# The second product of each attention block on the full array, with k's low part padded by zeros

## The chip, the core and the metric

The kernel runs on one core of a Trainium2 chip. The metric is the device time of one execution in microseconds; the runs shown are whole executions on the chip. The core has five engines that work beside each other, each through its own queue in a fixed order: TensorE (matmuls, and as a second queue the loads of their weights), VectorE, ScalarE, GpSimd and SyncE, which issues the transfers.

## The reference

The reference is an encoder of two layers on 512 tokens with 1024 features, in float32. Each layer has three branches that read the same normed stream: a neighbourhood attention on a 64 wide grid (4 heads), a sliding-window attention (8 query heads on 2 key heads, 128 queries per block), and a gated delta net run in both directions. The branches are projected, gated, added and projected again, and a feed-forward part follows. The change touches the logits of both attentions:

```python
s = jnp.einsum('brqhd,brjkhd->brhqjk', qg, kg).astype(jnp.float32) * (HEAD_DIM ** -0.5)     # neighbourhood
s = jnp.einsum('bnqhgd,bnkhd->bnhgqk', qb, kb).astype(jnp.float32) * (HEAD_DIM ** -0.5)     # sliding window
```

Both contract over the 64 features of a head.

## The kernel before, in words

Tokens lie along the columns and features on the 128 partitions. Every product of float32 values is made in three: a value is split into a rounded high part and a low part that holds the rest, and high x high, high x low and low x high are added in PSUM. For the weights `load_w` does this (lines 133 to 146): a transfer brings a chunk, ScalarE rounds it (line 142), GpSimd subtracts (line 144). `mm3` (lines 148 to 152) issues the three matmuls of 512 columns each; these are the bulk of the kernel's work (lines 150, 151, 152).

For the attentions a head has 64 features, so two heads share the partitions. For each of the two heads, e, `na_project` builds the stationary operand `qp[e]` with the head's q rounded on its own 64 partitions and q's low part on the other 64 (lines 376 and 377), and the moving operand `kh[e]` with k's rounded part on both halves. One product on the full array then gives q high x k high + q low x k high. The third term, q high x k low, is a second matmul into the same PSUM bank. It uses the 64 partitions of that head alone, with `kl`, one tile for both heads (line 380):

```python
T.matmul(sc[:, 0:256], lhsT=q_, rhs=kh[e][:, k1:k1 + 256], start=True, stop=False)
T.matmul(sc[:, 0:256], lhsT=q_[r], rhs=kl[r, k1:k1 + 256], start=False, stop=True)
```

These are lines 418 and 419 in `na_attend`, which runs over 2 pairs of heads, 4 blocks of 128 queries and the 2 heads of a pair: 16 times a layer, always 256 columns. In `swa_attend` lines 508 and 509 do the same for the sliding window, with `qs`, `kdh` and `kdl` from `swa_project`, over 4 query heads of a group, 4 blocks and 2 groups: 32 times a layer, with 256 columns at the ends and 384 between. VectorE then scales, masks and reduces the logits (lines 421 and 512), ScalarE takes the exponentials, TensorE transposes them (lines 430, 431, 530) and multiplies by v on half of the array's columns (lines 437, 534).

The delta net runs beside this. `gdn_cross` doubles k into tiles of the ring `dup` (`doubled`, by ScalarE at line 80), `gdn_solve` inverts the blocks by 31 steps of substitution on VectorE (lines 712 and 714) and transposes them (lines 721 to 727), and hands them to many small matmuls on parts of the array (line 748 on). `gdn_mid` transposes the doubled k (line 782) and the doubled v, which takes tiles of the same ring (lines 799 and 802). `gdn_scan` then goes through 8 steps in which TensorE and VectorE take turns (lines 831, 834, 842, 847). The merge (`merge`) issues the gates' and branches' dense products.

The order in which each engine meets its instructions is not that of the source. The program is traced in the order of the list `ORDER`, and a planner with its own estimates of durations then places instructions on the queues, so that the branches and the merge are mixed. Tiles of one name form a ring with as many buffers as `CAPS` gives; a new tile waits until the last reader of the buffer's old one is done.

Of the kernel before, what the change touches and what calls it, by code (L numbers as in the profile page):

```python
# [7 lines left out]
F32 = mybir.dt.float32  # L8
F32R = mybir.dt.float32r
# [12 lines left out]
# columns of the constant block  # L22
# [3 lines left out]
# columns of the parameter block  # L26
# [3 lines left out]
# chunks of the weight stream  # L30
# [19 lines left out]
CAPS |= {"ysh": 2, "ysl": 2, "kE": 4, "kT": 4, "Q": 4, "VN": 4, "SA": 4, "kq": 4, "dup": 6, "spr": 4, "xo": 4, "qs0": 4, "qs1": 4, "kdh0": 1, "kdh1": 1, "kdl": 1, "nkl": 2, "sv": 1, "hf": 8}  # L50
# [11 lines left out]
def encoder_kernel(ctx, tc, xT, wall, par, cst, nab, out, depth=2, dbg=None):  # L62
# [26 lines left out]
    # rings of 4 KB and 2 KB buffers, one of each for every line of work that runs beside the others  # L89
# [17 lines left out]
    # ---- constants, parameters and small values: one place for each name, or one of a ring  # L107
# [14 lines left out]
    # parameters of a layer  # L122
# [42 lines left out]
    # 1 / sqrt(a) up to the factor RSQ: the halved and inverted exponent as the start, three Newton steps  # L165
# [9 lines left out]
    # sums over the features (their halves), by token: [128, 4, 2]  # L175
# [10 lines left out]
    # values by token, [128, 4, n], brought back over the features  # L186
# [9 lines left out]
    # The residual stream arrives tile by tile: gained and split for the next products, its  # L196
    # squares summed; 1/rms is applied where the products leave PSUM.
# [77 lines left out]
    for l in range(depth):  # L275
# [9 lines left out]
        # raw projections normed over their heads  # L285
# [18 lines left out]
        def perm(a):   # token order (r c) seen as (c r)  # L304
            return a.rearrange("p (r c) -> p c r", r=8)
# [17 lines left out]
        def doubled(src):      # [128, 4, 64] -> the same twice, side by side  # L323
            t = tmp(shape=(128, 4, 2, 64), name="dup")
            (G.tensor_copy(t, src.unsqueeze(2).to_broadcast([128, 4, 2, 64])) if ENG.get("dup") == "G" else copy("dup", t, src.unsqueeze(2).to_broadcast([128, 4, 2, 64])))
            return t
# [11 lines left out]
        def by4(name):      # by chunk and head  # L338
            us = [tmp(shape=(128, 2, 4, 64), name=name) for _ in range(4)]
            return lambda n: us[n // 2][:, n % 2], us  # L340

        def by2(name):      # the same in four parts
            us = [tmp(shape=(128, 4, 2, 64), name=name) for _ in range(4)]
            return lambda n, h: us[n // 4 * 2 + h // 2][:, n % 4, h % 2], us

        def na_project():
            line[0] = "n"
            nonlocal naqk, vt, vt4, rns, irn
            # sums of squares of the stream, permuted
# [10 lines left out]
            for j in range(2):  # L360
                qn, kn = tmp(name="qn"), tmp(name="kn")
                vn = tmp(name="nav")
                acc = dense(l, CH_NA + 3 * j, h)
                S.activation(out=cr(qn), in_=perm(acc), func=AF.Copy, scale=P[:, P_QK:P_QK + 1])
                sq = tmp(name="sq")
                S.activation(out=cr(sq), in_=perm(acc), func=AF.Square)
                pb = sums(sq, halves, "at")
                V.tensor_tensor(anv[:, :, 2 * j:2 * j + 2], mp.unsqueeze(2).to_broadcast([128, 4, 2]),
                                pb, op=ALU.add)
                knorm(permuted(dense(l, CH_NA + 3 * j + 1, h), tmp(name="raw")), P[:, P_QK + 1:P_QK + 2], kn)  # L370
                qp, kh, kl = pair(F32R, name="nqs"), pair(F32R, name="nkh"), tmp(F32R, name="nkl")
                naqk.append((qp, kh, kl))
                for e in range(2):
                    r = slice(64 * e, 64 * e + 64)
                    o = slice(64 - 64 * e, 128 - 64 * e)
                    S.activation(out=qp[e][r], in_=qn[r], func=AF.Copy)
                    on("nql", "G").tensor_tensor(qp[e][o], qn[r], qp[e].bitcast(F32)[r], op=ALU.subtract)
                    copy("nkh", kh[e][r], kn[r], "V")
                    S.activation(out=kh[e][o], in_=kn[r], func=AF.Copy)
                    on("nkl", "V").tensor_tensor(kl[r], kn[r], kh[e].bitcast(F32)[r], op=ALU.subtract)  # L380
                permuted(dense(l, CH_NA + 3 * j + 2, h), vn)
                pt = bank("at")
                for b in range(4):
                    k0, kn0 = (0, 64) if b == 0 else (128 * b - 64, 128)
                    T.transpose(pt[0:kn0, 128 * b:128 * b + 128], vn[:, k0:k0 + kn0], ident)
                S.activation(out=vt[j][0:64, 0], in_=pt[0:64, 0:128], func=AF.Copy)
                S.activation(out=vt[j][:, 1:4], in_=pt[:, 128:512].rearrange("p (b m) -> p b m", b=3), func=AF.Copy)
                pt = bank("at")
                T.transpose(pt[0:64, 0:128], vn[:, 448:512], ident)
                S.activation(out=vt4[0:64, j], in_=pt[0:64, 0:128], func=AF.Copy)  # L390
# [6 lines left out]
        def na_attend():  # L397
            line[0] = "n"
            # ================= neighbourhood attention =================
            for j in range(2):  # L400
                qp, kh, kl = naqk[j]
                py = bank("at")
                for b in range(4):
# [5 lines left out]
                    # the scaled and biased logits negated, and the least of them  # L409
# [4 lines left out]
                    for e in range(2):  # L414
                        r = slice(64 * e, 64 * e + 64)
                        sc = bank("at")
                        q_, k1 = qp[e][:, 128 * b:128 * b + 128], min(k0, 256)
                        T.matmul(sc[:, 0:256], lhsT=q_, rhs=kh[e][:, k1:k1 + 256], start=True, stop=False)
                        T.matmul(sc[:, 0:256], lhsT=q_[r], rhs=kl[r, k1:k1 + 256], start=False, stop=True)
                        c0 = 4 * b + 2 * j + e  # L420
                        V.tensor_tensor_reduce(out=lg[:, e, 0:w], in0=sc[:, k0 - k1:k0 - k1 + w], in1=bias[:, e, 0:w], scale=rns[:, c0:c0 + 1],
                                               scalar=-NEG, op0=ALU.add, op1=ALU.min, accum_out=mx[:, e:e + 1])
# [21 lines left out]
        def swa_project():  # L444
# [5 lines left out]
            kdh, kdl = pair(F32R, name="kdh"), tmp(F32R, name="kdl")  # L450
            for gq in range(2):
# [4 lines left out]
                V.tensor_tensor(kdl[r], kr[r], kdh[gq].bitcast(F32)[r], op=ALU.subtract)  # L456
# [6 lines left out]
            # q stays as projected, times its gain; 1/rms goes into the exponentials  # L463
            qs = []
            aq = kept("aq")      # (b, head of the group, group)
# [23 lines left out]
        def swa_attend():  # L489
            line[0] = "a"  # L490
            # ================= sliding window attention =================
            y["s"] = [None] * 4
            for ep in range(2):
# [3 lines left out]
                for b in range(4):  # L497
# [3 lines left out]
                    for e in range(2):  # L501
                        c0 = 8 * b + 4 * ep + 2 * e
                        mx, sk = small(2, "s", 8), slice(4 * ep + 2 * e, 4 * ep + 2 * e + 2)
                        for gq in range(2):
                            sc = bank("at")
                            q_, kc = qs[2 * ep + e][gq][:, 128 * b:128 * b + 128], slice(128 * kb0, 128 * kb1)
                            r = slice(64 * gq, 64 * gq + 64)
                            T.matmul(sc[:, 0:w], lhsT=q_, rhs=kdh[gq][:, kc], start=True, stop=False)  # L508
                            T.matmul(sc[:, 0:w], lhsT=q_[r], rhs=kdl[r, kc], start=False, stop=True)  # L509
                            # the scaled and masked logits negated, and the least of them and of the sink  # L510
# [30 lines left out]
        def gdn_gates():  # L541
            line[0] = "g"
            nonlocal dec, egn, tlb, gh, gl, beta
            # ================= gated delta net =================
# [3 lines left out]
            # 16 columns beside 512: four parts of the contraction in four column groups, added on the way to the tokens  # L548
# [21 lines left out]
            # beta = 1 / (1 + exp(-b))  # L570
# [4 lines left out]
            # g = -exp(a_log) * (max(a, 0) + log1p(exp(-|a|)))  # L575
# [13 lines left out]
            # cumulative decays  # L589
# [8 lines left out]
            # g split for the decay matrices  # L598
# [5 lines left out]
        def gdn_project():  # L604
            line[0] = "g"
            nonlocal bk, ik, kq, vs, kss, qss
            # k, q, v, twice what the short convolution and silu give. The norms of k and q are applied
            # later: 1/|k| squared in beta, |k| in v, and |q| beside the eps of the output norm.
# [14 lines left out]
            for c in range(2):  # L623
# [9 lines left out]
                if c == 0:  # L633
                    # by token of a chunk, for both directions
# [14 lines left out]
        def gdn_cross():  # L649
            line[0] = "g"  # L650
            nonlocal Q, Qu, Xo, Xg, Lt, Rt, kds, qdec
            # X = beta_j (k_j . k_i) decay, Q = beta_j (q_i . k_j) decay, rows j, columns i
# [4 lines left out]
            for hh in range(4):  # L657
# [24 lines left out]
                # the blocks on the diagonal, column by column, and those beside it  # L682
# [11 lines left out]
        def gdn_solve():  # L694
            line[0] = "g"
            nonlocal W
            # W = (I + X)^-1: the 32-blocks of the diagonal by substitution, one block per lane
# [17 lines left out]
            # back: W[j, i] (forward: R[i, j], backward: R[j, i])  # L715
# [22 lines left out]
            # off-diagonal: W12 = -W11 X12 W22 (forward), W21 = -W22 X21 W11 (backward)  # L738
# [32 lines left out]
        def gdn_mid():  # L771
            line[0] = "g"
            nonlocal kE, kT, wn, VN
            # k and v by token, in both halves of the partitions
# [11 lines left out]
            # wn = -(W' kE)^T rows dk, u = W' v rows i  # L786
# [29 lines left out]
        def gdn_scan():  # L816
            line[0] = "g"
            nonlocal SA
            # scan; VN holds u and then the new values
# [31 lines left out]
        def gdn_z():  # L851
            line[0] = "g"
            nonlocal zs
            # z, twice its silu
# [7 lines left out]
        def gdn_out():  # L862
            line[0] = "g"
            # ---- delta net: outputs, gated RMS norm
# [23 lines left out]
        def merge(i, bn):  # L888
            line[0] = "m"
            # ================= merge =================  # L890
# [49 lines left out]
        # ================= feed forward =================  # L940
# [39 lines left out]
def _w_chunks(w_in, w_bn, w_bs, w_bg, w_out, w_up, w_down):  # L980
# [6 lines left out]
    def put(c, w):      # w: [d, K, 128]  # L987
# [143 lines left out]
```

## Time and profile before

| | |
|---|---|
| median of 3 runs | 1728.22 us (1725.38 to 1728.62) |
| profiled execution: first to last instruction | 1725.9 us |
| TensorE busy | 1685.1 us, 98% |
| weight loads busy | 1329.0 us, 77% |
| VectorE busy | 1009.2 us, 58% |
| GpSimd busy | 832.5 us, 48% |
| ScalarE busy | 743.6 us, 43% |
| mean granted TensorE clock | 0.985 |

The profile comes from one execution. For it the page gives the span from the first to the last instruction and no time around it; the lowest of the runs lies 0.5 us below this span and the median 2.3 us above. A matmul's end in the profile is modelled, so a busy TensorE isn't one at its peak; the distance from one start to the next tells more. In a row, "L509" is line 509 of the kernel, "PE" TensorE, "PEld" its weight loads, "DVE" VectorE, "ACT" ScalarE, "POOL" GpSimd; "64*128 64x256" is a stationary operand of 64 rows and 128 columns and a moving one of 64 rows and 256 columns.

### The profile page before, as it was taken

How to read it: one execution, taken by the hardware profiler on the slowest of the kernel's cores; microseconds unless marked ns; L12 is line 12 of the kernel's file. 1: busy time of each engine (PE TensorE's matmuls, PEld its weight loads, DVE VectorE, ACT ScalarE, POOL GpSimd, SP SyncE). 2: the span in 40 equal slices, each digit the busy share in tenths (PEclk: the TensorE clock that was granted, in tenths of full speed). 3: DMA queues.
4: the chain of work that ended last, by engine and by line, in shares of the span. 5: the costliest groups of instructions: out<-in, count | busy, mean ns of one | idle time of the engine just before them, and what ended most of it. 6: DMA issues, size and time to landing. Idle time of an engine off the chain costs nothing.

```text
span 1725.9 us, 25175 instructions
## 1 busy us (share of the span) xinstructions
PE 1685.1 (98%) x9196; PEld 1329.0 (77%) x9196; DVE 1009.2 (58%) x1809; ACT 743.6 (43%) x1436; POOL 832.5 (48%) x740
## 2 busy tenths in 40 slices
PE   7989999999999999999999999999999999999999
PEld 5766767677888888878886776677778888888887
DVE  5599895434547777741126898855355477777300
ACT  5545544423445444443335564544234354444321
POOL 4664441264544555554448553412644545555543
PEclk9999999999999999999999999999999999999999
DMA  6222221122452332334333221110224623333332
GB/s 209 80 60 75 67 64 36 37 69 70 133 188 87 97 98 98 98 114 132 119 98 95 70 65 49 56 41 29 76 84 143 193 75 96 98 98 98 127 123 74
DMA packets 91500, 160.46 MB, mean 93 GB/s; under 512 B 10352, under 2 KB 17136, under 8 KB 91376
## 3 DMA queue, kind: packets, MB, share of 16 engines
q1 hardware_dynamic: 91376, 158.85, 29.0%
q8 instruction: 72, 1.18, 0.3%
q14 instruction: 52, 0.43, 0.1%
HBM read 147.80 MB, written 8.39 MB: 90 GB/s over the span
## 4 chain that ended last, share of the span: by engine, by line
PE 85%; DVE 9%; issue 2%; ACT 2%; POOL 1%; DMA 1%; SPq 0%; DVEq 0%; POOLq 0%; ACTq 0%
PE mm L152 25%; PE mm L150 24%; PE mm L151 24%; PE at L534 1%; PE at L530 1%; PE at L509 1%; PE at L508 1%; DVE qd L666 1%; PE gd L842 1%; DVE fix L172 1%; DVE fix L170 1%; PE gd L831 1%; PE gd L811 1%; POOL wl L144 1%; DVE lg L427 1%
## 5 line engine op out<-in xcount | busy, mean ns | idle before, releaser
L144 POOL TENSOR_TENSOR wl<-wr,wh 128x512 fp32r<-128x512 f32 (+1 forms) x512 | 686.8, 1349 | 806.8 <-ACT wh L142 754.1
L150 PE MATMUL mm<-hh,wh 128*128 128x512 f32 x1408 | 560.6, 398 | 13.3 <-ACT wh L142 11.7
L152 PE MATMUL mm<-hh,wl 128*128 128x512 f32 x1408 | 561.2, 400 | 1.9 <-POOL wl L144 1.7
L151 PE MATMUL mm<-hl,wh 128*128 128x512 f32 x1408 | 557.2, 396 | 0.0
L142 ACT ACTIVATE wh<-wr 128x512 fp32r<-128x512 f32 (+1 forms) x512 | 314.0, 618 | 402.9 <-PE mm L151 256.1
L150 PEld LDWEIGHTS mm<-hh,wh 128*128 128x128 f32 x1408 | 268.4, 191 | 72.0 <-ACT wh L142 14.3
L152 PEld LDWEIGHTS mm<-hh,wl 128*128 128x128 f32 x1408 | 268.1, 190 | 65.8 <-POOL wl L144 5.7
L151 PEld LDWEIGHTS mm<-hl,wh 128*128 128x128 f32 x1408 | 267.8, 190 | 58.4 <-issue 2.4
L234 DVE SCALAR_TENSOR_TENSOR cv<-up,fix,cv 128x511 f32<-128x511 f32 x88 | 142.0, 1613 | 2.8
L152 PE MATMUL mm<-act,wl 128*128 128x512 f32 x352 | 137.3, 390 | 0.6 <-POOL wl L144 0.6
L150 PE MATMUL mm<-act,wh 128*128 128x512 f32 x352 | 137.2, 390 | 0.3 <-ACT wh L142 0.3
L233 DVE SCALAR_TENSOR_TENSOR cv<-up,fix,cv 128x511 f32<-128x511 f32 x88 | 85.8, 974 | 88.1 <-ACT cv L232 88.1
L151 PE MATMUL mm<-act,wh 128*128 128x512 f32 x352 | 137.1, 389 | 0.0
L970 DVE TENSOR_TENSOR xo<-xo,mm 128x512 f32<-128x512 f32 x16 | 11.0, 687 | 192.1 <-PE mm L152 192.1
L232 ACT ACTIVATE cv<-up,fix 128x512 f32<-128x512 f32 x88 | 70.8, 809 | 34.7 <-DVE up L280 34.7
L162 ACT ACTIVATE act<-cv 128x512 fp32r<-128x512 f32 x44 | 27.8, 632 | 125.8 <-DVE cv L953 125.8
L152 PEld LDWEIGHTS mm<-act,wl 128*128 128x128 f32 x352 | 66.1, 188 | 15.1 <-POOL wl L144 1.5
L150 PEld LDWEIGHTS mm<-act,wh 128*128 128x128 f32 x352 | 66.1, 188 | 14.2 <-ACT wh L142 0.7
L151 PEld LDWEIGHTS mm<-act,wh 128*128 128x128 f32 x352 | 66.1, 188 | 13.8
L952 ACT ACTIVATE cv<-cv 128x512 f32<-128x512 f32 x44 | 27.8, 633 | 85.9 <-DVE cv L234 85.9
L280 DVE TENSOR_TENSOR up<-mm,rstd 128x512 f32<-128x512 f32 x88 | 59.5, 680 | 8.2 <-ACT rstd L228 8.2
L512 DVE CUSTOM_DVE_ANT_0 spr<-at,fix 128x256 f32<-128x256 f32 (+1 forms) x64 | 38.4, 607 | 34.1 <-PE at L509 33.4
(283 smaller groups left out, 2231.7 us busy)
## 6 DMA issues: line engine op xcount, KB each, us to landing
wr<-in_wall_dram SPq DMA_DIRECT2D x496, 256.0 KB, 2.7
xs<-xo SPq DMA_DIRECT2D x24, 256.0 KB, 2.8
xo<-xs SPq DMA_DIRECT2D x24, 256.0 KB, 3.6
xo<-in_xT_dram SPq DMA_DIRECT2D x16, 256.0 KB, 5.2
sw<-raw SPq DMA_DIRECT2D x40, 64.0 KB, 2.0
wr<-in_wall_dram SPq DMA_DIRECT2D x16, 128.0 KB, 3.0
out_dram<-xo SPq DMA_DIRECT2D x8, 256.0 KB, 2.3
nab<-in_nab_dram SPq DMA_DIRECT2D x8, 248.0 KB, 2.7
```

The lines of the kernel that those rows point to most:

```text
L142: S.activation(out=hi[:, :n], in_=raw[:, :n], func=AF.Copy)
L144: G.tensor_tensor(lo[:, :n], raw[:, :n], hi.bitcast(F32)[:, :n], op=ALU.subtract)
L150: T.matmul(acc, lhsT=wh, rhs=rh, start=start, stop=False)
L151: T.matmul(acc, lhsT=wh, rhs=rl, start=False, stop=False)
L152: T.matmul(acc, lhsT=wl, rhs=rh, start=False, stop=stop)
L162: S.activation(out=hi, in_=src, func=AF.Copy)
L232: S.activation(out=dst, in_=src, func=AF.Identity, scale=w[:, 1:2], bias=bias)
L233: V.scalar_tensor_tensor(dst[:, 1:L], src[:, 0:L - 1], w[:, 0:1], dst[:, 1:L], op0=ALU.mult, op1=ALU.add)
L234: V.scalar_tensor_tensor(dst[:, 0:L - 1], src[:, 1:L], w[:, 2:3], dst[:, 0:L - 1], op0=ALU.mult, op1=ALU.add)
L280: V.tensor_tensor(dst, acc, rstd, op=ALU.mult)
L512: V.tensor_tensor_reduce(out=pr[:, 0:w], in0=sc[:, 0:w], in1=smask[:, 128 * (b == 0):128 * (b == 0) + w], scale=rqs[:, c0 + gq:c0 + gq + 1 ...
L952: S.activation(out=cv[0], in_=cv[0], func=AF.Silu)
```

## The change

The second product uses all 128 partitions. k's low part gets a tile for each head (or group) instead of one for both: the head's 64 partitions hold the low part, the other 64 are set to zero by GpSimd. The zeros meet q's low part and add nothing. This takes 3 more tiles of 2 KB a partition, less one: the ring `dup` goes from 6 to 5. Comments were dropped too. Cut to its core:

```diff
-CAPS |= {..., "dup": 6, ..., "kdl": 1, "nkl": 2, "sv": 1, "hf": 8}
+CAPS |= {..., "dup": 5, ..., "kdl0": 1, "kdl1": 1, "nkl0": 2, "nkl1": 2, "sv": 1, "hf": 8}
...
-                qp, kh, kl = pair(F32R, name="nqs"), pair(F32R, name="nkh"), tmp(F32R, name="nkl")
+                qp, kh, kl = pair(F32R, name="nqs"), pair(F32R, name="nkh"), pair(F32R, name="nkl")
...
-                    on("nkl", "V").tensor_tensor(kl[r], kn[r], kh[e].bitcast(F32)[r], op=ALU.subtract)
+                    on("nkl", "V").tensor_tensor(kl[e][r], kn[r], kh[e].bitcast(F32)[r], op=ALU.subtract)
+                    G.memset(kl[e].bitcast(F32)[o], 0.0)
...
-                        r = slice(64 * e, 64 * e + 64)
...
-                        T.matmul(sc[:, 0:256], lhsT=q_[r], rhs=kl[r, k1:k1 + 256], start=False, stop=True)
+                        T.matmul(sc[:, 0:256], lhsT=q_, rhs=kl[e][:, k1:k1 + 256], start=False, stop=True)
...
-            kdh, kdl = pair(F32R, name="kdh"), tmp(F32R, name="kdl")
+            kdh, kdl = pair(F32R, name="kdh"), pair(F32R, name="kdl")
...
-                V.tensor_tensor(kdl[r], kr[r], kdh[gq].bitcast(F32)[r], op=ALU.subtract)
+                V.tensor_tensor(kdl[gq][r], kr[r], kdh[gq].bitcast(F32)[r], op=ALU.subtract)
+                G.memset(kdl[gq].bitcast(F32)[o], 0.0)
...
-                            r = slice(64 * gq, 64 * gq + 64)
...
-                            T.matmul(sc[:, 0:w], lhsT=q_[r], rhs=kdl[r, kc], start=False, stop=True)
+                            T.matmul(sc[:, 0:w], lhsT=q_, rhs=kdl[gq][:, kc], start=False, stop=True)
```

## Rows read from the trace of the kernel before

**Rows 1.** The page: TensorE's busy time, and the chain that ended last, by engine.

```profile
PE 1685.1 (98%) x9196; PEld 1329.0 (77%) x9196; DVE 1009.2 (58%) x1809; ACT 743.6 (43%) x1436; POOL 832.5 (48%) x740
...
PE 85%; DVE 9%; issue 2%; ACT 2%; POOL 1%; DMA 1%; SPq 0%; DVEq 0%; POOLq 0%; ACTq 0%
```

**Rows 2.** Stretches: length; PE, PEld, DVE, ACT, POOL busy us; clock; DMA share; GB/s.

```profile
100.00:257.00 157.00, 152.35 (x768) 111.59 (x767) 143.43 (x328) 85.84 (x198) 78.09 (x111) 0.98 0.22 67
257.00:345.00 88.00, 88.00 (x895) 64.39 (x895) 47.62 (x145) 43.73 (x114) 16.77 (x16) 0.96 0.12 37
957.00:1113.00 156.00, 150.20 (x741) 110.65 (x743) 138.55 (x323) 85.03 (x194) 78.02 (x108) 0.97 0.19 60
```

**Rows 3.** TensorE's timeline, single rows: start, us, instruction, [idle before, releaser].

```profile
99.16 1.09 PE L193 MATMUL at<-fix,rb 128*128 128x128 f32 x4 [5.95 <-DVE rb L190]
...
256.94 3.80 PE L748 MATMUL gd<-WT,Xo 32*32 32x32 f32 x128 [1.87 <-DVE fix L512]
...
276.58 1.09 PE L782 MATMUL gd<-fix,dup 128*128 128x128 f32 x8
...
302.02 0.66 PE L802 MATMUL gd<-fix,dup 128*128 128x128 f32 x4
...
1112.78 3.83 PE L748 MATMUL gd<-WT,Xo 32*32 32x32 f32 x128 [2.04 <-DVE fix L512]
```

**Rows 4.** Line 509 alone, by stretch: length; PE and PEld busy us; clock.

```profile
257.00:345.00 88.00, 8.09 (x20) 3.66 (x20) 0.96 0.12 37
```

**Rows 5.** Lines 509 and 419: ns min/median/max, first and last start, shapes.

```profile
L509 PE MATMUL at<-kdl,qs x64: 378/435/579, 206.8 to 1198.7; 64*128 64x256 f32 x32, 64*128 64x384 f32 x32
...
L419 PE MATMUL at<-nkl,nqs x32: 378/381/580, 119.7 to 1060.2; 64*128 64x256 f32 x32
```

**Rows 6.** TensorE's timeline: a pair between full products, and one between column-tiled groups.

```profile
322.19 0.39 PE L152 MATMUL mm<-hh,wl 128*128 128x512 f32 x1
322.41 0.33 PE L508 MATMUL at<-kdh,qs 128*128 128x384 f32 x1
...
323.04 0.50 PE L150 MATMUL mm<-hh,wh 128*128 128x512 f32 x1
323.38 0.39 PE L151 MATMUL mm<-hl,wh 128*128 128x512 f32 x1
...
324.24 0.50 PE L152 MATMUL mm<-hh,wl 128*128 128x512 f32 x1
324.67 0.65 PE L534 MATMUL at<-th,sv 128*64 128x256 f32 x4
325.25 0.45 PE L508 MATMUL at<-kdh,qs 128*128 128x384 f32 x1
...
325.99 0.65 PE L534 MATMUL at<-th,sv 128*64 128x256 f32 x4
```

**Rows 7.** The weight loads behind a 64-row product, and the next one.

```profile
226.51 0.19 PEld L152 LDWEIGHTS mm<-hh,wl 128*128 128x128 f32 x1 [0.19 <-issue]
226.62 0.19 PEld L150 LDWEIGHTS mm<-hh,wh 128*128 128x128 f32 x1
```

**Rows 8.** VectorE's waits: first layer's stretch, then the second's; us, times, longest.

```profile
DVE nav L311 <- PE mm L152: 0.4, 1, 0.4
...
DVE lg L421 <- PE at L419: 2.0, 3, 0.9
...
DVE y L441 <- ACT y L440: 1.5, 2, 1.2
```

**Rows 9.** Memsets on GpSimd: ns min/median/max, first and last start, shapes.

```profile
L706 POOL MEMSET Rt<- x2: 955/967/979, 189.6 to 1040.9; 128x1024 f32 x2
...
L822 POOL MEMSET SA<- x2: 309/309/309, 251.4 to 1107.3; 64x256 f32 x2
```

**Rows 10.** ScalarE's timeline: the second early copy of v into the ring dup.

```profile
162.48 0.62 ACT L80 ACTIVATE dup<-vs 128x512 f32<-128x512 f32 x1
```

**Rows 11.** The stretch in which TensorE waited for rows 3's first entry (columns as rows 2).

```profile
95.50:102.30 6.80, 3.14 (x26) 2.34 (x26) 6.52 (x23) 4.13 (x10) 4.12 (x3) 0.50 0.17 45
```

More of the change, by code (lines that the diff above doesn't have):

```diff
@@ L49 @@
                               ("qd", 2), ("wn", 2), ("vs", 1), ("z", 1), ("act", 22)) for i in "01"}
-CAPS |= {"ysh": 2, "ysl": 2, "kE": 4, "kT": 4, "Q": 4, "VN": 4, "SA": 4, "kq": 4, "dup": 6, "spr": 4, "xo": 4, "qs0": 4, "qs1": 4, "kdh0": 1, "kdh1": 1, "kdl": 1, "nkl": 2, "sv": 1, "hf": 8}
+CAPS |= {"ysh": 2, "ysl": 2, "kE": 4, "kT": 4, "Q": 4, "VN": 4, "SA": 4, "kq": 4, "dup": 5, "spr": 4, "xo": 4, "qs0": 4, "qs1": 4, "kdh0": 1, "kdh1": 1, "kdl0": 1, "kdl1": 1, "nkl0": 2, "nkl1": 2, "sv": 1, "hf": 8}
 ORDER = "np na sp sa gg gp gx gs gm gc gz go mn ms mg"
```

## The prediction

> **What bounds the kernel now.** I read the page's first part and its chain of waits first. The reader is to see that TensorE is called busy for 98% of the span and carries 85% of the chain that ended last, VectorE 9% [rows 1]. That is an average, so I then read busy time by stretch, in the stretches where the changed products lie [rows 2]. Each layer has two of them, parted by the moment at which VectorE hands the solved blocks of the delta net to TensorE (matmuls of line 748, at 256.9 and 1112.8 us). Before it VectorE is busy 143.4 of 157 us, and 138.6 of 156 in the second layer: both engines are full, and VectorE's own queue leads to line 748, for which TensorE stands still for 1.87 us [rows 2, 3]. Behind it VectorE has work for 47.6 of 88 us, and TensorE for all of them [rows 2]. So a nanosecond saved on TensorE counts in full behind line 748 and for little ahead of it.
>
> Then I counted the changed products by stretch: line 509 runs 64 times, 32 in a layer, and 20 of the first layer's stand behind line 748; line 419 runs 32 times, 16 in a layer, the last at 1060.2 us, so all of them before [rows 4, 5]. That is 28 products of a layer before line 748 and 20 behind.
>
> **What one 64-row product costs.** The product's own matmul isn't slow; its neighbours are. In the timeline of TensorE a matmul of 512 columns on the full array starts 0.22 us after the one before it (322.19 to 322.41). The lone pair behind it takes 322.41 to 323.04, 0.63 us for twice 384 columns, and the full product that follows takes 0.34 us to the next start instead of 0.22 to 0.23 (323.04 to 323.38) [rows 6]. The weight queue shows why: behind a 64-row product the next load begins after an idle 0.19 us, while between two full ones the loads begin 0.11 us apart, beside a running matmul [rows 7]. The array's rows are regrouped on the way in and again on the way out, and each time a load of 0.19 us and the emptying of the array stand bare.
>
> **The change, part by part.** *The product on the full array.* No row shows a fp32 product of 256 or 384 columns in an unbroken full-array stream. Its step is bounded below by the 0.11 us between loads and above by the 0.22 us of 512 columns; I take the columns' share, 0.17 us for 384, which is nearest to the upper row. A pair between full matmuls then costs 2 x 0.17 = 0.34 in place of 0.63 + 0.11 = 0.74 us: **0.40 us** saved. If what follows is a matmul on a part of the array (lines 534, 748, 763, 793, 811), the array still has to be regrouped. A full matmul ahead of such a group starts it 0.43 us later where 0.34 would do (324.24 to 324.67), so that costs 0.09. A pair between two groups of line 534 takes 0.74 us now (325.25 to 325.99) [rows 6]; it would take 0.34, 0.11 for its first bare load and 0.09, so 0.54: **0.20 us** saved. For 256 columns I take the same savings, since load and emptying don't grow with the columns (an estimate).
>
> Along TensorE's timeline I counted what follows each run of such pairs. Behind line 748, 12 of the 20 pairs of a layer end against a part of the array, 8 don't: 12 x 0.20 + 8 x 0.40 = 5.6 us a layer, **11.2 us** in both. Before it, 6 of 28 do in the first layer and 3 of 28 in the second: 10.0 and 10.6 us, **20.6 us**, but there VectorE decides. Bounds for what of the 20.6 arrives: 0 and 20.6. VectorE is idle for 13.6 us of the first layer's stretch, but only 0.4 of it is a wait for TensorE; in the second it waits 2.0 us for line 419 and 1.5 for a ScalarE step that follows TensorE [rows 2, 8]. I take 0.5 and 3.0: **3.5 us**, nearest to those rows. The rest becomes a longer wait of TensorE at line 748.
>
> A rule that speaks against the change: the Trainium skill, "TensorE: Matmul & The Clock Gate", Part 3 (packing small matmuls), says that a weight load runs beside matmuls in flight only when its row group differs from theirs. By it a full-array pair would pay each load bare, as the pair does now, and the saving would be about 0. The trace doesn't agree: with 0.19 us loads the full matmuls still start 0.22 us apart. So the sum above keeps the rows' value.
>
> *The zeros.* Four memsets of 64 x 512 in the neighbourhood projection and two in the window projection of each layer, 12 in all, on GpSimd. Two rows bracket one: 0.31 us for 256 columns and 0.97 for 1024 [rows 9]; on the line between them 512 take 0.53, so 6.4 us of GpSimd. Nothing has to be computed for them, and GpSimd is busy half of the stretch, 78.1 of 157 us [rows 2]; that is the cover. Behind them in its queue stand the low halves of the weights (line 144), for which TensorE waits, so the bounds are 0 and 6.4; a gain is excluded, as no work goes. I take **1 us** of loss. The products' new wait for a memset costs nothing, since they wait already for the subtractions of the same projection, and the first of line 419 starts only at 119.7 us [rows 5]; without that cover it would be one memset, 0.53 us.
>
> *The ring "dup" goes from 6 to 5 buffers.* Four hold k until line 782 has read them, from 276.6 us on [rows 3]; now two copies of v are made early, the second at 162.5 us, and with five buffers that one must wait for line 782. It takes 0.62 us on ScalarE and is first needed by the second group of line 802, at 302.0 us [rows 3, 10]. Some 25 us of cover: **0**, and up to 0.62 a layer if it is gone.
>
> *Order.* A planner that estimates times orders the queues, and new memsets and buffers can move its choices; no row prices that. I take 0 and leave 5 us each way for the range.
>
> **Sum.** 11.2 + 3.5 - 1 = 13.7 us. The profiled execution spans 1725.9 us, which gives 1712.2. The median of the runs is 2.3 us above that span, so I predict **1714.5 us**, 0.8% less. A measurement of this kernel tells a change of about 0.2%, or 3.5 us, from none.
>
> **Rivals.** *The gain ahead of line 748 arrives too* (20.6 instead of 3.5), because the freed TensorE time there lets merge work run earlier that now lies behind. For it: TensorE carries 85% of the chain [rows 1]. Against it: VectorE is busy for 143.4 of 157 us there [rows 2]. In full it gives 1697, at half 1706. Chance 0.17.
>
> *New waits take the gain behind line 748.* The pairs are filler between steps of the delta net's scan, in which TensorE and VectorE answer each other; with shorter filler the answers come late. If 10 of 11.2 us go so, 1725. For it: the scan's shape. Against: TensorE shows no idle time there, and VectorE is idle for almost half of it [rows 2]. Chance 0.10, of which half would count as no change.
>
> *Slower, by the clock.* TensorE waited 5.95 us up to 99.16, and from 95.5 to 102.3 us the granted clock was 0.50, the lower of its two levels (1.2 in place of 2.4 GHz) [rows 3, 11]. The wait of 1.87 us at line 748 would grow by up to 9 us a layer, and earlier waits appear. A half-clock stretch of 6.8 us costs up to 3.4 us where TensorE decides; from five more of them there, the 13.7 us are gone, and six cost 20.4: 1735. Against: ahead of line 748 TensorE has room for them. Chance 0.07.
>
> *It doesn't do what it says:* the second product reads the same queries as the first, and its load may still begin only when the first product's matmul is done. Then a pair costs 0.74 us as now, nothing is saved, and 1 us of memsets is lost: 1729. Against it stand the loads 0.11 us apart between full matmuls [rows 7]. The skill's rule on loads, above, would give the same. Chance 0.03.
>
> **How the numbers follow.** The forecast has 0.63, with its own range of 1707 to 1721 from the order's 5 us and the bounds of memsets and waits. The 8-in-10 range takes in the first rival from its half upwards and part of the second: **1700 to 1725**. Faster: 0.63 + 0.17 + 0.04 = 0.84. No change: 0.06 of the second rival and 0.03 of the fourth, less a little: 0.08. Slower: 0.08, the clock and an order that went wrong.
>
> **What would show it.** In the changed profile: the second products as 128 x 256 and 128 x 384; the loads between two products of a pair 0.11 to 0.17 us apart with no idle time; a lone pair in a full stream in about 0.34 us; a longer wait ahead of line 748 and a span from there to the layer's end shorter by about 5.6 us. Wrong is the working if the pairs still take 0.6 us, if the wait at line 748 doesn't grow while the whole gains over 20 us, or if new waits of TensorE appear in the scan.

## The result, and the profile after

The changed kernel takes **1710.57 us**, median of 4 runs (1708.84 to 1713.21), against 1727.85 (1725.38 to 1728.62) for the kernel before on the same chip: a ratio of 0.9897 [0.9883, 0.9910], 17.3 us or 1.0% less. The profiled execution took 1711.75 us and spans 1710.0. Behind the edits line numbers are one higher than before, so 748 is now 749, 842 is 843 and the two products are lines 420 and 510.

The page of the changed kernel: span, busy times, and the chain that ended last.

```profile
span 1710.0 us, 25217 instructions
...
PE 1656.6 (97%) x9196; PEld 1319.6 (77%) x9196; DVE 1008.1 (59%) x1809; ACT 739.1 (43%) x1436; POOL 834.5 (49%) x752
...
PE 79%; DVE 14%; issue 3%; ACT 2%; DMA 1%; POOL 0%; SPq 0%; DVEq 0%; ACTq 0%; POOLq 0%
```

Against [rows 1], TensorE does the same 9196 matmuls in 28.5 us less, and VectorE's part of the chain rises from 9 to 14%. So not all of those 28.5 us arrived. The stretches show where (columns as in [rows 2]; the first and third lie ahead of the hand-over at line 749, the second behind it).

```profile
100.00:259.00 159.00, 147.92 (x766) 111.63 (x766) 144.88 (x331) 85.44 (x197) 81.36 (x115) 0.96 0.22 68
259.00:341.50 82.50, 82.35 (x899) 62.84 (x899) 47.97 (x148) 43.77 (x116) 17.95 (x18) 0.96 0.12 40
955.00:1105.00 150.00, 138.33 (x730) 106.04 (x728) 135.38 (x316) 82.20 (x189) 77.52 (x108) 0.99 0.20 62
```

Ahead of the hand-over in the first layer TensorE's idle time grew from 4.65 us (157.00 less 152.35) to 11.08, and the stretch is no shorter: VectorE is as busy as it was. Behind it TensorE is busy throughout, as before. TensorE's timeline gives the ends of the stretches exactly: the hand-over in each layer, then line 843 in the third of the scan's 8 steps, which stands behind the layer's last changed product, so that the stretch behind the hand-over can be closed there.

```profile
259.03 3.81 PE L749 MATMUL gd<-WT,Xo 32*32 32x32 f32 x128 [2.72 <-DVE fix L513]
...
341.47 1.14 PE L843 MATMUL gd<-VN,kT 64*64 64x64 f32 x16
...
1104.99 3.80 PE L749 MATMUL gd<-WT,Xo 32*32 32x32 f32 x128 [4.53 <-DVE fix L513]
...
1187.39 1.13 PE L843 MATMUL gd<-VN,kT 64*64 64x64 f32 x16
```

Against [rows 3], the wait at the hand-over went from 1.87 to 2.72 and from 2.04 to 4.53 us. In the kernel before, the third step comes at 345.85 and 1203.31:

```profile
345.85 1.13 PE L842 MATMUL gd<-VN,kT 64*64 64x64 f32 x16
...
1203.31 1.13 PE L842 MATMUL gd<-VN,kT 64*64 64x64 f32 x16
```

From that the change of the span by stretch, in us (before, after):

| stretch | before | after | change |
|---|---|---|---|
| start to first hand-over | 256.94 | 259.03 | +2.1 |
| behind it, to the scan's third step | 88.91 | 82.44 | -6.5 |
| third step to the second hand-over | 766.93 | 763.52 | -3.4 |
| behind it, to the scan's third step (second layer) | 90.53 | 82.40 | -8.1 |
| rest | 522.6 | 522.6 | 0.0 |

The sum is -15.9; the other 1.4 us of the 17.3 lie between span and median. Of the third line, -3.6 stand in the second layer's stretch ahead, from its wait at line 193 to the hand-over (159.0 to 155.5 us). VectorE's waits there answer to [rows 8]:

```profile
DVE y L442 <- ACT y L441: 1.2, 1, 1.2
...
DVE lg L422 <- PE at L420: 0.2, 1, 0.2
```

Its wait for the neighbourhood logits fell from 2.0 to 0.2 us, and the ScalarE step from 1.5 to 1.2. The single products look as the working had them. TensorE's timeline, a pair inside a stream of full products and one between column-tiled groups, as in [rows 6]:

```profile
320.15 0.33 PE L509 MATMUL at<-kdh,qs 128*128 128x384 f32 x1
320.32 0.34 PE L510 MATMUL at<-kdl,qs 128*128 128x384 f32 x1
320.49 0.40 PE L150 MATMUL mm<-hh,wh 128*128 128x512 f32 x1
320.73 0.39 PE L151 MATMUL mm<-hl,wh 128*128 128x512 f32 x1
...
322.22 0.44 PE L509 MATMUL at<-kdh,qs 128*128 128x384 f32 x1
322.50 0.34 PE L510 MATMUL at<-kdl,qs 128*128 128x384 f32 x1
322.77 0.65 PE L535 MATMUL at<-th,sv 128*64 128x256 f32 x4
```

In the stream the pair takes 320.15 to 320.49, 0.34 us, and the next product starts 0.24 later; before it was 0.63 and 0.34. Between column-tiled groups it is 0.55 in place of 0.74. The weight queue, as in [rows 7], shows the loads 0.11 to 0.18 us apart, each 0.19 long, with no idle time:

```profile
224.01 0.19 PEld L509 LDWEIGHTS at<-kdh,qs 128*128 128x128 f32 x1
224.12 0.19 PEld L510 LDWEIGHTS at<-kdl,qs 128*128 128x128 f32 x1
224.30 0.19 PEld L509 LDWEIGHTS at<-kdh,qs 128*128 128x128 f32 x1
```

Last, the two products and the memsets by line (ns min/median/max, first and last start, shapes), the memsets as in [rows 9]:

```profile
L510 PE MATMUL at<-kdl,qs x64: 277/308/342, 207.5 to 1182.9; 128*128 128x256 f32 x32, 128*128 128x384 f32 x32
...
L420 PE MATMUL at<-nkl,nqs x32: 277/280/415, 121.7 to 1054.0; 128*128 128x256 f32 x32
...
L382 POOL MEMSET nkl<- x8: 518/519/773, 1.9 to 948.7; 64x512 f32 x8
...
L458 POOL MEMSET kdl<- x4: 518/518/520, 0.7 to 337.5; 64x512 f32 x4
```

### The profile page after: what moved, and what is told of

It is laid out like the page before. It is cut to its first block, busy times and chain, and to the rows that moved or that the text cites. A ratio compares the mean times of both kernels' runs of the same rounds, so it can differ in the third digit from the quotient of the medians.

```text
span 1710.0 us, 25217 instructions
## 1 busy us (share of the span) xinstructions
PE 1656.6 (97%) x9196; PEld 1319.6 (77%) x9196; DVE 1008.1 (59%) x1809; ACT 739.1 (43%) x1436; POOL 834.5 (49%) x752
## 4 chain that ended last, share of the span: by engine, by line
PE 79%; DVE 14%; issue 3%; ACT 2%; DMA 1%; POOL 0%; SPq 0%; DVEq 0%; ACTq 0%; POOLq 0%
PE mm L152 23%; PE mm L150 23%; PE mm L151 23%; DVE Rt L715 1%; DVE Tm L713 1%; PE at L535 1%; PE at L531 1%; DVE qd L667 1%; DVE lg L428 1%; DVE fix L172 1%; PE gd L843 1%; PE gd L832 1%; DVE fix L170 1%; PE gd L812 1%; PE at L509 1%
## 5 line engine op out<-in xcount | busy, mean ns | idle before, releaser
L150 PEld LDWEIGHTS mm<-hh,wh 128*128 128x128 f32 x1408 | 268.0, 190 | 74.2 <-ACT wh L142 15.9
L150 PEld LDWEIGHTS mm<-act,wh 128*128 128x128 f32 x352 | 66.1, 188 | 14.2 <-ACT wh L142 0.7
L151 PEld LDWEIGHTS mm<-act,wh 128*128 128x128 f32 x352 | 66.1, 188 | 13.7
L900 ACT ACTIVATE gt<-gt 128x512 f32<-128x512 f32 x48 | 30.2, 630 | 66.4 <-DVE gt L280 66.3
```

The costliest lines, as they stand in the source:

```text
L150: T.matmul(acc, lhsT=wh, rhs=rh, start=start, stop=False)
L151: T.matmul(acc, lhsT=wh, rhs=rl, start=False, stop=False)
L900: S.activation(out=gt[q], in_=gt[q], func=AF.Tanh, scale=0.5)
```

## The experiments

Two theories at the start. **Mine:** the products gain what full-array steps save, behind the hand-over in full; padding and ring are worth nothing or cost 1 us. **The rivals:** a part of the gain is made by the moved copy in the ring, by the padding, or ahead of the hand-over by freed TensorE time.

In the padding alone, its repeat, the change's repeat and the two runs with one product, every engine meets its instructions in the sequence of the changed kernel, so that they differ in the products alone; the ring alone has that sequence without the memsets. In all other runs below the planner also put instructions elsewhere, from some 120 of TensorE's matmuls (two and two) to some 1400 (both divisions on ScalarE), so their times hold a change of order too.

**The padding alone.** Both second products back on 64 rows of the padded tiles:

```
-  T.matmul(sc[:, 0:256], lhsT=q_, rhs=kl[e][:, k1:k1 + 256], ...)
+  T.matmul(sc[:, 0:256], lhsT=q_[64*e:64*e+64], rhs=kl[e][64*e:64*e+64, k1:k1 + 256], ...)
-  T.matmul(sc[:, 0:w], lhsT=q_, rhs=kdl[gq][:, kc], ...)
+  T.matmul(sc[:, 0:w], lhsT=q_[64*gq:64*gq+64], rhs=kdl[gq][64*gq:64*gq+64, kc], ...)
```

> The kernel before with the padded tiles, the 12 memsets and the ring of 5, but the second products still on 64 rows. Theory (all of the gain is the products'; zeros and ring cost 1 to 2 us): 1728.5 to 1730.5 us against 1727.9 before. Rival 1 (the copy moved by the smaller ring, or the new order, gives part of the gain): below 1725. Rival 2 (the zeros cost more, and the products gave more than the 17 us seen): above 1732. TensorE's pairs should stay at 0.63 us in a full stream.

Measured: 1725.4 us against 1728.0, 0.9987 [0.9979, 0.9996]. The expectation missed by some 3 us: twelve memsets of 0.52 us cost nothing that shows, and the kernel is, if anything, 2.6 us faster. TensorE's pairs in a full stream stay at 0.63 us.

**One product at a time.** First the neighbourhood's alone (the window's back on 64 rows, the last edit above), then the window's alone (the first edit above).

> The changed kernel with the sliding window's second products back on 64 rows, so that only the neighbourhood attention's 32 run on the full array. All of them stand ahead of line 748. Theory (VectorE decides there; what arrives is the second layer's waits of VectorE for TensorE, some 3.5 us, less 1 to 2 for the zeros): 1724 to 1728. Rival (TensorE decides ahead of line 748 as well): 26 pairs x 0.4 + 6 x 0.2 = 11.6 us, less 1 to 2, so 1717 to 1718.

> The changed kernel with the neighbourhood attention's second products back on 64 rows, so that only the sliding window's 64 run on the full array: 40 behind line 748, 24 ahead. Theory: the stretches behind line 748 shorten as in the changed kernel (6.5 and 8.1 us in the profiles), ahead little: 1712 to 1715. Rival (TensorE decides everywhere): 11.2 behind and some 9 ahead, less the zeros: 1708 to 1709.

Measured: 1723.38, 0.9975 [0.9965, 0.9986], and 1712.89, 0.9917 [0.9903, 0.9930]. Against padding alone the neighbourhood's 32 products give 2.0 us, the window's 64 give 12.5, both 14.8: they add up. (The 2.0 is hardly clear of noise, as the two intervals overlap.) The neighbourhood's lie ahead of the hand-over and bring 2.0 of the 32 x 0.40 = 12.8 us they save at most; the rival, by which they arrive, falls. The windows from the hand-over to the scan's third step of the window-only kernel are those of the change:

```profile
259.36:341.97 82.61, 82.49 (x899) 62.95 (x899) 47.93 (x148) 43.73 (x116) 17.97 (x18) 0.96 0.12 40
1105.77:1188.18 82.41, 82.29 (x899) 63.04 (x899) 46.36 (x148) 43.60 (x115) 16.90 (x16) 0.96 0.12 40
```

**Fewer changes of the array, without padding.** In the kernel before, the order first, first, second, second in two banks:

```
+  for gq in range(2):
+      T.matmul(scs[gq][:, 0:w], lhsT=<all rows>, rhs=kdh[gq][:, kc], start=True, stop=False)
   for gq in range(2):
-      T.matmul(sc[:, 0:w], lhsT=q_, rhs=kdh[gq][:, kc], start=True, stop=False)
       T.matmul(scs[gq][:, 0:w], lhsT=<64 rows>, rhs=kdl[r, kc], start=False, stop=True)
```

> The kernel before, all second products on 64 rows of one tile, but in the order first, first, second, second for the two heads of a block (two banks), instead of first, second, first, second. Theory (each change between the full array and 64 rows costs, not the 64-row product): half of the changes go, so about half of the gain: 1717 to 1721, and two second products in a row start about 0.11 to 0.17 us apart. Rival (a 64-row product is slow by itself, its load never beside a matmul): no gain, 1726 to 1730, and second products in a row still 0.3 us apart or more.

Measured: 1724.36, 0.9978 [0.9969, 0.9987], 3.6 us. The planner kept only 26 of the 48 couples together, so that the array changes 70 times where it changed 96: 27% fewer, about a quarter of the 14.8 us. The time lies between the two forecasts. It fits a cost by change of array, but doesn't show it: only 4 of the 26 couples stand behind a hand-over, where a saving on TensorE counts, so 3.6 us is more than they can give at 0.40 us each, and the order of the queues changed too. TensorE's timeline:

```profile
209.52 0.48 PE L508 MATMUL at<-kdh,qs 128*128 128x256 f32 x2
209.94 0.38 PE L511 MATMUL at<-kdl,qs 64*128 64x256 f32 x2
210.25 0.38 PE L508 MATMUL at<-kdh,qs 128*128 128x256 f32 x1
210.56 0.38 PE L511 MATMUL at<-kdl,qs 64*128 64x256 f32 x1
210.87 0.33 PE L432 MATMUL at<-fix,lg 128*128 128x128 f32 x1
```

Two 64-row products on different halves of the rows take 209.94 to 210.25, 0.31 us together, as long as one alone (210.56 to 210.87). They run side by side.

**A full product more, ahead and behind.** In the changed kernel the low part is added twice, which counts it double in the logits: once for the neighbourhood, once for the window.

```
   T.matmul(sc[:, 0:256], lhsT=q_, rhs=kl[e][:, k1:k1 + 256], ...)
+  T.matmul(sc[:, 0:256], lhsT=q_, rhs=kl[e][:, k1:k1 + 256], ...)
```

> The changed kernel (1710.6 us), with each of the neighbourhood attention's 32 second products issued twice in a row (the low part is added twice): 32 x 0.12 = 3.8 us more for TensorE, all ahead of line 748. Theory (VectorE decides there, TensorE has slack): 0 to 1.5 us more, 1710.5 to 1712. Rival (TensorE's time ahead counts in full): 3.8 us more, 1714.4.

> The changed kernel, with each of the sliding window's 64 second products issued twice (the low part is added twice). Behind the hand-over to TensorE stand 24 of 256 columns and 16 of 384: 24 x 0.12 + 16 x 0.175 = 5.7 us; ahead the other 24, 8 x 0.12 + 16 x 0.175 = 3.8 us. Theory (only what lies behind counts): 5.7 to 7 us more than the changed kernel's 1710.6, 1716 to 1718. Rival 1 (all counts): 9.5 more, 1720. Rival 2 (in the scan TensorE waits for VectorE's answers, which hides it): below 1713.

Measured: 1712.23 and 1717.38, so 1.7 and 6.8 us above the change. The first is 0.2 us over its theory, the second within. Thirty-two products ahead cost 0.05 us each on the median, and nothing in the profile: the hand-overs stand at 259.82 and 1105.07, and the span is 1710.3 against 1710.0. Sixty-four window products, 40 of them behind, cost 6.8. By the forecast's steps these 40 make 5.7 of it (24 of 256 columns, 16 of 384); where the other 1.1 lie isn't shown. The profile doesn't split it by layer either: the stretch behind grew by 3.9 us in the first layer and by 0.2 in the second, in which the fall of the clock lies ahead of the hand-over (from 1094.1 us) instead of behind it. The step of a full product of 384 columns in TensorE's timeline is the 0.17 us of the prediction:

```profile
317.97 0.34 PE L510 MATMUL at<-kdl,qs 128*128 128x384 f32 x1
318.14 0.34 PE L511 MATMUL at<-kdl,qs 128*128 128x384 f32 x1
318.32 0.34 PE L509 MATMUL at<-kdh,qs 128*128 128x384 f32 x1
```

**The ring alone.** In the kernel before `"dup": 6` becomes `"dup": 5`.

> The kernel before with the ring of doubled tiles cut to 5 and nothing else. The run with the padded tiles alone came out 2.6 us below the kernel before, though zeros can only cost. Theory (the second copy of v, which the ring of 5 moves from 162 to 287 us, frees ScalarE where VectorE waits for it): 1724.5 to 1726.5 against 1728.0. Rival (it came from the new alignment of GpSimd's work with VectorE's, or from the clock): 1727 to 1729.

Measured: 1728.15, 0.9997 [0.9983, 1.0010]. The ring costs and gains nothing; that the moved copy makes part of the gain falls.

**The padding again, and the change again**, with no new edit, to see what repeats:

> The padded tiles alone once more, beside the changed kernel and the one before. If the 2.6 us that this gained the first time come from the zeros' new place in GpSimd's queue, it is again 1.5 to 3.5 us below the kernel before; if they were the spread of the runs, within 1 us of it. In its profile the stretches behind the hand-over show the second fall of the clock, some 15 us behind it, in about 5 of 8 cases (the 64-row products of the window), so in one or two of the two.

> The changed kernel once more: 1709 to 1712, 14 to 17 us below the padded tiles alone. In its profile no second fall of the clock in the stretches behind the hand-over, and both of them 82 to 83 us long; if the clock has nothing to do with the products, one of the two shows it and is 2 to 2.5 us longer.

Measured: 1725.15, 0.9982 [0.9972, 0.9992], and 1710.71, 0.9898 [0.9881, 0.9916]. The gain of the products themselves is 14.4 us here, 14.8 above; padding alone is again about 3 us below the kernel before. The change's stretches are 82.2 and 82.4 us long without a second fall of the clock, as expected; the padding's profile, for which one or two second falls were expected, shows none.

**Where the clock comes in.** The windows from the hand-over to the scan's third step show a second fall of the clock that I hadn't looked for. Kernel before:

```profile
256.94:345.85 88.91, 88.79 (x898) 64.84 (x899) 48.47 (x148) 43.87 (x115) 16.83 (x16) 0.96 0.11 37
1112.78:1203.31 90.53, 90.42 (x898) 66.16 (x899) 47.90 (x148) 43.80 (x114) 16.80 (x16) 0.93 0.11 36
...
1129.80:1136.50 6.70, 6.70 (x27) 4.94 (x24) 5.88 (x17) 2.52 (x7) 0.00 (x0) 0.50 0.00 0
```

Ring alone:

```profile
257.34:348.32 90.98, 90.86 (x898) 66.18 (x899) 47.83 (x148) 44.49 (x116) 16.85 (x16) 0.92 0.11 36
1114.60:1205.09 90.49, 90.37 (x899) 66.05 (x899) 47.86 (x148) 44.38 (x115) 16.86 (x16) 0.93 0.11 36
```

Padding alone, second profile:

```profile
257.87:345.98 88.11, 88.00 (x898) 64.18 (x898) 48.59 (x148) 44.42 (x116) 17.91 (x18) 0.96 0.12 37
1111.64:1199.29 87.65, 87.53 (x899) 64.09 (x899) 47.04 (x148) 44.34 (x115) 16.87 (x16) 0.96 0.12 37
```

The change again:

```profile
258.98:341.17 82.19, 82.07 (x899) 62.66 (x899) 47.94 (x148) 43.73 (x116) 17.97 (x18) 0.96 0.12 40
1104.48:1186.85 82.37, 82.25 (x898) 63.01 (x898) 46.36 (x148) 43.59 (x115) 16.94 (x16) 0.96 0.13 40
```

In nearly every stretch the granted clock is at its lower level, 0.50, for some 7 us about the hand-over. With a mean of 0.96 that is all. In the kernel before it falls a second time, from 1129.8 to 1136.5, with TensorE busy throughout; the mean is then 0.93 and the stretch longer. Among the 10 stretches with 64-row window products in the old order (before, ring, padding twice, neighbourhood alone) five show the second fall: a mean of 88.2 us for those without it and 90.8 with it, so 2.6 us each. With two and two it is in neither of two. Among the 16 with full window products (this kernel twice, and six of the experiments) it is in none.

That the 64-row products bring it about is not shown by this. Only six of the 16 (the change, its repeat, the window alone) have the sequence of instructions of the ten, and five of ten against none of six is little. Nor do the whole executions bear it out: their mean granted clock was 0.9854 to 0.9861 in the groups of the kernel before, 0.9870 and 0.9873 with the padding alone, 0.9865 and 0.9872 in the change. So the 14.8 and 14.4 us between padding and change came at about the same clock. What the clock gives lies between the kernel before and the padding, where the products are still on 64 rows.

**Other work put on the full array.** In the changed kernel the product of window weights and values, two column-tiled products of 256 columns, becomes one of 512 on the full array, of which two quarters are read (ring at 4):

```
-  for gq in range(2):
-      T.matmul(py[64*gq:64*gq+64, 0:256], lhsT=vst[:, <64 columns>], rhs=pT[:, <256 columns>], ..., tile_position=(0, 64*gq))
+  T.matmul(py, lhsT=vst[:, 128 * kb:128 * kb + 128], rhs=pT, ...)
```

> The changed kernel, in which the sliding window's products with v also use the full array: one matmul of 512 columns for both groups in place of two of 256 on half the columns of the array (half of its output is not used), with the output read in two pieces and the ring of doubled tiles at 4. Theory (each change of the array's partition costs 0.1 to 0.2 us, and the 80 steps over key blocks lose about 0.13 us each, some 6 of 10 us of it behind line 748): 1703 to 1707. Rival (two products on half the columns run side by side, 0.11 us for both, so the full product's 0.22 us eats the gain): 1709 to 1713.

Measured: 1726.2, 0.9992 [0.9982, 1.0002], 15.6 us above the change: 80 matmuls fewer (each product stands as two rows in the trace), and a time as before the change. Its timeline:

```profile
289.72 1.13 PE L534 MATMUL at<-th,sv 128*128 128x512 f32 x2
290.68 0.60 PE L531 MATMUL at<-fix,spr 128*128 128x128 f32 x4
```

One such product, in its two rows, takes 0.96 us to the next start; the two column-tiled ones of the change, in four rows with as many columns in all, take 0.58 (288.26 to 288.84). So column groups run side by side in part, and here the tiles pay. How much of the 15.6 us that makes isn't shown: the stretches behind the hand-overs are 5.6 and 2.5 us longer, but another 4.3 lie behind the second of them, where few of these products stand, and the ring, the output read in two pieces and the order changed as well.

**Who decides ahead of the hand-over.** In the changed kernel, the division of the neighbourhood's weights from VectorE to ScalarE; then the window's division (line 525) as well:

```
-  on("lg", "V").tensor_scalar(lg[:, e, 0:w], lg[:, e, 0:w], rs[:, e:e + 1], None, op0=ALU.mult)
+  S.activation(out=lg[:, e, 0:w], in_=lg[:, e, 0:w], func=AF.Copy, scale=rs[:, e:e + 1])
```

> The changed kernel, with the division of the neighbourhood attention's weights by their sum (line 428, 16 pairs of instructions in all, some 10 us a layer) moved from VectorE to ScalarE. Theory (VectorE decides ahead of line 749, where TensorE now waits 10 us a layer): the hand-over comes 3 to 7 us earlier in each layer, 1697 to 1705. Rival (the step lies in a chain from exponential to transposition, and ScalarE's queue is what makes VectorE wait): no gain, 1709 or more.

> As the run before it, and the sliding window's division (line 525, 64 instructions of 0.34 to 0.41 us) on ScalarE too. Of these 24 stand ahead of the hand-over, 9 us in both layers. Theory: as the run before it or 1 to 4 us better, 1694 to 1704. Rival: ScalarE becomes what the scan waits for, and it is worse than the run before it by 2 us or more.

Measured: 1704.7, 0.9864 [0.9847, 0.9881], **faster than both kernels**, and 1718.86, 0.9946 [0.9930, 0.9963]. With the first edit the stretches ahead are 154.9 and 154.2 us long (159.0 and 155.5 in the change) and those behind stay:

```profile
253.81:336.38 82.57, 82.45 (x899) 63.19 (x899) 47.97 (x148) 43.55 (x116) 17.92 (x18) 0.95 0.13 40
1098.97:1182.21 83.24, 83.12 (x899) 63.56 (x899) 46.23 (x148) 43.67 (x116) 16.82 (x16) 0.94 0.13 39
```

So VectorE's work decides ahead, though less than forecast: the stretch became 4.1 us shorter in the first layer and 1.3 in the second, not 3 to 7 in each. With both edits the theory missed and the rival's sign came, 14.2 us more than the run before. The stretches behind grow by 5.1 and 4.0 us, while VectorE has 10 us less to do in the first of them and ScalarE 8.9 more:

```profile
252.43:340.11 87.68, 87.68 (x914) 66.61 (x913) 38.02 (x118) 52.46 (x133) 18.91 (x18) 0.95 0.12 37
```

But the rival's reason is not what the trace shows: TensorE is busy throughout and waits for ScalarE nowhere there, while VectorE waits 15.7 us for line 510. What grew is TensorE's own time; the planner had put some 15 more matmuls behind the hand-over (914 in place of 899). So this run doesn't tell what the second division itself is worth.

## Why the prediction came out right, and where its terms were off

**One pair: right.** It took 0.34 us for a pair in a full stream and 0.54 between column-tiled groups; the rows show 0.34 and 0.55. The chosen step of 0.17 us for 384 columns, between ends of 0.11 and 0.22, is what the timeline and the doubled window product show.

The rule weighed there, that a load runs beside matmuls only when its row group differs (the Trainium skill, "TensorE: Matmul & The Clock Gate", Part 3), would have left the pair at 0.74 us. The loads of full-array products 0.11 to 0.18 us apart disagree, and so does the gain.

**Behind the hand-over: the size of the term held, and a side effect was missing.** 5.6 us a layer was predicted. Without a second fall of the clock the stretches went from a mean of 88.2 to 82.4 (six of the change, its repeat and the window alone), which is 5.8. The second layer gave 8.1: in its profile the second fall of the clock went too, 2.5 us. The prediction read the clock only as a rival that makes the kernel slower, with TensorE standing still as its ground; the fall that mattered lay in a stretch where TensorE never stands still, and the profile of the change doesn't have it. **This is what the working lacked**, and the largest part of the distance between 13.7 and 15.9 us of span. Whether it went by the products or by chance is open, as said above.

**Ahead of the hand-over: right in kind, off in the first layer.** The prediction took 3.5 of 20.6 us as arriving: 0.5 and 3.0. The second layer gave 3.6 (2.5 against the padding alone, 158.0 to 155.5). The first gave nothing: its stretch between the wait at line 193 and the hand-over is 159.0 us, 158.4 in the repeat, with 157.8 before; 158.2 with the ring alone and 158.3 to 158.6 with the padding alone. So the saving there is within what moves from kernel to kernel.

The prediction let the rest become a longer wait at line 748. The wait grew, but took only 0.85 of the 6.4 us by which TensorE's idle time rose in the first layer's stretch. Most of the rest became waits for VectorE and ScalarE inside the attentions. TensorE's waits before, then after:

```profile
PE at L430 <- DVE lg L427: 1.5, 2, 0.9
...
PE at L431 <- DVE lg L428: 2.6, 2, 2.0
...
PE at L531 <- DVE spr L525: 1.7, 1, 1.7
```

The wait at line 531 is new, as is one of 1.2 us for ScalarE at line 535.

**The zeros: the price of one was right, the cost to the kernel wrong.** A memset takes 0.52 us (0.53 predicted), 12 of them 6.3 us of GpSimd. The 1 us of loss stood for the work behind them; up to line 193 the change is 0.85 us later, but padding alone is 2.6 and 3.4 us *faster*. Fewer second falls would give a part of that: one in four of its stretches, three in four of the kernel before and the ring alone. The mean clocks above agree: they are 0.0009 and 0.0018 higher with the padding, and among the executions of the kernel before in these two groups 0.001 goes with 1.6 and 1.2 us, so by estimate the clock gives 1.4 of the 2.6 us and 2.1 of the 3.4. Why the clock is higher there is open.

**The ring: right.** The early copy of [rows 10] went from 162.5 to 276.9, when line 783 begins to read; the last of the four copies starts at 284.0, and the second group of line 803 at 301.1 without a wait. **The order: right**; on TensorE and VectorE the instructions stand in the same sequence before and after, and only that copy and the 12 memsets differ.

**The rivals.** That the gain ahead arrives too is refuted by the neighbourhood alone (2.0 us), by its doubling and by the move to ScalarE. No new wait showed in the scan. "It doesn't do what it says" fell with the first timeline. The forecast of 1714.5 was 3.9 us too high: of that, in these two profiles, 2.5 are the clock, 0.9 the first layer behind, 0.6 the second ahead, 1.7 the place of the median in relation to the span, less 1.6 ahead in the first layer and 0.2 elsewhere.

## What to carry to other kernels

Price a small product by the gap it leaves for its neighbours: a lone 64-row product among full ones cost 0.40 us of regrouping, and zeros in the unused rows removed that at 0.52 us of an engine with time to spare. Tiles that follow each other in groups are the opposite case: there a full product took 0.96 us where two tiled ones took 0.58. Count a saving only in the stretches where its engine decides; where another engine does, move that engine's work.

## What was not expected of the hardware

- The clock can fall to its lower level while TensorE is busy without a gap (1129.8 to 1136.5 us, busy 6.70 of 6.70), and that took 2.6 us.
- Two 64-row products on different halves of the array took 0.31 us together, as long as one. The Trainium skill, "TensorEngine Tiling (Array Packing)", Key Properties, says that tiles operate independently and that a change of the tiling mode drains the engine; both agree with this row and with the 0.40 us of a lone pair.
- VectorE is held by GpSimd. In its timeline the same instructions take 0.68 and 0.41 us, or 1.78 and 1.50:

```profile
16.75 0.68 DVE L211 TENSOR_TENSOR hl<-hf,hh 128x512 fp32r<-128x512 f32 x1
17.35 0.41 DVE L210 CAST hh<-hf 128x512 fp32r<-128x512 f32 x1
...
18.29 1.78 DVE L211 TENSOR_TENSOR hl<-hf,hh 128x512 fp32r<-128x512 f32 x1
19.99 1.50 DVE L210 CAST hh<-hf 128x512 fp32r<-128x512 f32 x1
```

```profile
17.95 3.25 POOL L144 TENSOR_TENSOR wl<-wr,wh 128x512 fp32r<-128x512 f32 x2 [3.22 <-DMA fix<-in_cst_dram]
```

Over the whole trace of the changed kernel 187 of VectorE's 1809 instructions last over 0.6 us longer than the shortest of their line and form. Beside every one of them runs a two-input operation of GpSimd (beside one of them a memset as well); of the 1062 instructions with no such operation beside them, none is that long. Where the two meet shifts with every edit to GpSimd's queue, which may be why the first wait at line 193 ends between 97.9 and 100.9 us in the runs with padding, and between 98.6 and 99.2 in the three without (not tested). The Trainium skill, "SBUF — State Buffer", Who interferes with whom, says that a VectorE instruction with two inputs contends with a GpSimd instruction that reads, not with one that only writes; the trace agrees for line 211, which has two inputs. Line 210 has one, and is held as well.
